# Level products of the gated recurrences as four 64 by 64 tiles

## The chip, the cores and the metric

The kernel runs on one NeuronCore of a Trainium2 chip. The metric is the device time of one execution in microseconds. The core has five engines with in-order instruction queues: TensorE (PE; its weight loads are shown apart as PEld), VectorE (DVE), ScalarE (ACT), GpSimd (POOL) and SyncE (SP), which issues most of the DMAs.

## What is computed

One layer of a decoder trunk over 2048 tokens of width 1024, in f32: a token mixer (three groups of heads in parallel), then a gated MLP with a short convolution, each between an adaLN-conditioned RMSNorm and a gated residual, and a last RMSNorm. Two of the head groups are gated recurrences, HGRN2 (8 heads, key width 64) and GLA (4 heads, key width 32), with a decay per key channel and token:

```python
def step(s, inp):                       # one chunk of tokens
    qn, kn, vn, gn = inp                # gn: log of the decay
    cum = jnp.cumsum(gn, axis=2)
    rel = jnp.where(causal, cum[:, :, :, None, :] - cum[:, :, None, :, :], -jnp.inf)
    attn = jnp.einsum('bhid,bhjd,bhijd->bhij', qn, kn, jnp.exp(rel))
    o = jnp.einsum('bhij,bhje->bhie', attn, vn) + jnp.einsum('bhid,bhde->bhie', qn * jnp.exp(cum), s)
    last = cum[:, :, -1:, :]
    s_new = jnp.exp(last[:, :, 0, :])[..., None] * s + jnp.einsum('bhjd,bhje->bhde', kn * jnp.exp(last - cum), vn)
    return s_new, o
```

The third group, retention (4 heads, key width 64), has a fixed decay per head.

## The kernel before

Tokens are worked in four blocks of 512 (`TB`), each as four chunks of 128 (`NCH`). Projections, the output projection and the MLP are products in three passes over a high and a low part of each operand (`split3`, lines 256 to 258); they make up most of TensorE's queue. The mixer's recurrences are woven into that queue by hand. A `Clock` counts the microseconds of TensorE work that the program has emitted so far (`adv`), and a recurrence is a generator that yields how many microseconds of other work should come before its next step. `clock.chain` runs such generators one after another. Within one engine the order is the order of emission, except that `tc.high_priority(offset=n)` moves instructions ahead by n places in the count of instructions.

`gated` is the generator for one unit: two HGRN2 heads (`unit_h`, 4 units a block, 16 in all) or the four GLA heads (`unit_g`, 1 a block, 4 in all; two "subs" of two heads that share keys and decays). Channels lie on the 128 partitions, 64 for each of two heads, tokens along the free axis. The decayed scores inside a chunk are built by levels. First, pairs of neighbouring tokens (`near`, `dots`). Then for each span s = 2, 4, 8, 16, 32, 64 (`LEVELS`) the scores of the tokens in the second half of each block of 2s against the keys of its first half: a product, a masked copy of it into the score tile `at` (line 679 on VectorE for s up to 16, line 676 on ScalarE above), and a multiplication of the queries (line 668) and the keys (line 670) by the decay of the span. The queries and keys thus change between levels, and the next level's product waits for both.

A level's product (line 660) is one f32 matmul for each chunk: 128 keys as weights, all 128 channels contracted, and as moving operand the queries of half the tokens for both heads side by side, 128 columns. To keep the heads apart the query tile `qbd` has double width and block-diagonal content: `[P, 2, TB]`, where GpSimd clears the half that belongs to the other head (`new_qbd`, lines 532 and 534). For GLA the rows outside the sub's heads are cleared too. After the last level ScalarE copies the second head's rows into the first half (line 691), so that `q[:, 0, :]` holds both heads for the product with the state (line 592).

Scores go to PSUM banks of the tag `lev`, of which there are two. An HGRN2 level writes one bank, a GLA level two, one for each sub. The retention units (`retention`) use the same tag, with one bank for each head, and products over 64 partitions (line 899). They also take their query tile from the tag `qbd`. `kT`, `u` and the outputs use the tag `late`, projections the tag `acc`.

Of the kernel before, what the change touches and what calls it, by code (L numbers as in the profile page):

```python
# [10 lines left out]
F32 = mybir.dt.float32  # L11
# [4 lines left out]
ALU = mybir.AluOpType  # L16
PSUM = bass.MemoryType.PSUM

P = 128
# [3 lines left out]
TB = 512  # L23
NB = SEQ // TB
NCH = TB // P
# [18 lines left out]
M_AT = {2: M_2, 4: M_4, 8: M_8, 16: M_16}  # L44
# [8 lines left out]
M512, M256, MF = 0.227, 0.12, 0.224  # L53
# [5 lines left out]
class Clock:  # L59
# [15 lines left out]
    def adv(self, us):  # L75
        self.t += us
        while self.due and self.due[0][0] <= self.t:
            self._next()
# [26 lines left out]
def trunk(ctx, tc, xT, vecs, cvec, cst, rope, msk, wada, win, walow, wgla, wout, wup, wdown, out):  # L105
# [14 lines left out]
    adv = clock.adv  # L120
# [4 lines left out]
    def lev_ps(name):  # L125
        return pp.tile([P, 512], F32, tag="lev", name=name, bufs=2)
# [133 lines left out]
    h = [None] * KD  # L260
# [264 lines left out]
                low(t[:], k)  # L525


    def new_qbd(name, rows):

        q = p1.tile([P, 2, TB], F32, tag="qbd", name="qb" + name, bufs=3)  # L530
        for hh in range(2):
            G.memset(q[64 * hh:64 * hh + 64, 1 - hh, :], 0.0)
            if rows[hh][1] - rows[hh][0] < 64:
                G.memset(q[64 * hh:64 * hh + 64, hh, :], 0.0)
        return q

    states = [p1.tile([P, NS, P], F32, tag=f"S{i}", name=f"S{i}") for i in range(7)]
    for st in states:
# [88 lines left out]
    def gated(name, b, ui, pos, kq, decay, subs, xy):  # L627

        Sst = states[ui]
        tree, cur = decay  # L630
        two = len(subs) > 1
        nh = 2 * len(subs)
        dots = pu.tile([P, NCH * nh, 2], F32, tag="dots", name="dot" + name, bufs=3)
        pss = [lev_ps(f"dt{name}_{t}") for t in range(2)]
        for ps, x in zip(pss, xy):
            for c in range(NCH):
                T.transpose(ps[:, c * P:(c + 1) * P], x[:, c * P:(c + 1) * P], ident)
        attns = []
        with tc.high_priority(offset=CHAIN):
            for t, ps in enumerate(pss):  # L640
                V.tensor_reduce(dots[:, :, t], ps[:].rearrange("p (a d) -> p a d", a=NCH * nh),  # L641
                                axis=mybir.AxisListType.X, op=ALU.add)
            for i, _ in enumerate(subs):
                at = pa.tile([P, 8 * P], F32, tag="a4k", name=f"at{name}_{i}")
                d8 = dots[:].rearrange("p (a i) t -> p a i t", i=len(subs))[:, :, i, :]
                mk = m_all[:, M_PAIR:M_PAIR + P].bitcast(F32).rearrange("p (n t) -> p n t", t=2)
                V.tensor_tensor(at[:].rearrange("p (a n t) -> p a n t", a=8, t=2),
                                d8.unsqueeze(2).to_broadcast([P, 8, 64, 2]),
                                mk.unsqueeze(1).to_broadcast([P, 8, 64, 2]), op=ALU.mult)
                attns.append(at)  # L650
        adv(4 * MF)
        yield PAIR_GAP
        for li, s in enumerate(LEVELS):
            nb = 64 // s
            pss = []
            for q, rows, v, sg in subs:
                ps = lev_ps(f"lv{name}_{s}")
                for c in range(NCH):
                    rhs = q[:, :, c * P:(c + 1) * P].rearrange("p h (n t s) -> p h n t s", t=2, s=s)[:, :, :, 1, :]
                    T.matmul(ps[:, c * P:(c + 1) * P].rearrange("p (h n s) -> p h n s", h=2, s=s),  # L660
                             kq[:, c * P:(c + 1) * P], rhs, start=True, stop=True)
                pss.append(ps)
            with tc.high_priority(offset=CHAIN):
                ev = tree[li]
                nn = TB // (2 * s)
                for q, rows, v, sg in subs:
                    qv = q[:].rearrange("p h (n t s) -> p h n t s", t=2, s=s)[:, :, :, 1, :]
                    V.tensor_tensor(qv, qv, ev[:, :, 0:1].unsqueeze(1).to_broadcast([P, 2, nn, s]), op=ALU.mult)
                kv = kq[:].rearrange("p (n t s) -> p n t s", t=2, s=s)[:, :, 0, :]
                V.tensor_tensor(kv, kv, ev[:, :, 1:2].to_broadcast([P, nn, s]), op=ALU.mult)  # L670
                for ps, at in zip(pss, attns):
                    dst = at[:].rearrange("p (a n t s) -> p a n t s", a=8, t=2, s=s)[:, :, :, 1, :]
                    src = ps[:].rearrange("p (a n s) -> p a n s", a=8, s=s)
                    if s >= 32:
                        for j0 in range(0, P, 2 * s):
                            S.copy(dst[j0:j0 + s, :, j0 // (2 * s), :], src[j0:j0 + s, :, j0 // (2 * s), :])
                    else:
                        mk = m_all[:, M_AT[s]:M_AT[s] + nb].unsqueeze(2).to_broadcast([P, nb, s])
                        V.copy_predicated(dst, mk.unsqueeze(1).to_broadcast([P, 8, nb, s]), src)
            adv(4 * len(subs) * MF)  # L680
            yield LEVEL_GAP[two]
        ps = late_ps("kT" + name)
        nk = NCH if b < NB - 1 else NCH - 1
        for c in range(nk):
            T.transpose(ps[:, c * P:(c + 1) * P], kq[:, c * P:(c + 1) * P], ident)
        kT = pu.tile([P, NCH, P], F32, tag="kT", name="kT" + name, bufs=1)
        with tc.high_priority(offset=CHAIN):
            S.copy(kT[:, 0:nk, :].rearrange("p c n -> p (c n)"), ps[:, 0:nk * P])
            for q, rows, v, sg in subs:
                r0, r1 = rows[1]  # L690
                S.copy(q[r0:r1, 0, :], q[r0:r1, 1, :])
        adv(4 * MF)
        yield 2.8 if two else 1.8
        while name not in tokens:
            yield 1.0
        for q, rows, v, sg in subs:
            ps = late_ps("u" + name)
            for c in range(nk):
                T.matmul(ps[:, c * P:(c + 1) * P], kT[:, c, :], v[:, c, :], start=True, stop=True)
            with tc.high_priority(offset=CHAIN):  # L700
                for c in range(nk):
                    for hh, (r0, r1) in enumerate(rows):
                        es = slice(64 * hh, 64 * hh + 64)
                        dst = Sst[r0:r1, (b * NCH + c + 1) % NS, es]
                        u = ps[r0:r1, c * P + hh * 64:c * P + hh * 64 + 64]
                        if b == 0 and c == 0:
                            V.tensor_copy(dst, u)
                        else:
                            V.scalar_tensor_tensor(dst, Sst[r0:r1, (b * NCH + c) % NS, es], cur[r0:r1, c:c + 1], u,
                                                   op0=ALU.mult, op1=ALU.add)  # L710
        adv(4 * len(subs) * MF)
        yield 4.0 if two else 2.2
        os = []
        for i, ((q, rows, v, sg), at) in enumerate(zip(subs, attns)):
            if i:
                yield 2.2
            o = pu.tile([P, NCH, P], F32, tag="o", name=f"o{name}_{i}")
            ps = attn_out(f"{name}_{i}", b, at, v, q[:, 0, :], Sst)
            adv(12 * MF)
            with tc.high_priority(offset=CHAIN):  # L720
                S.copy(o[:].rearrange("p c e -> p (c e)"), ps[:])
                post(o, sg, f"{name}_{i}")
            os.append(o)
        yield None
        for i, o in enumerate(os):
            yield 3.0 if i else POST_GAP
            transposed(b, pos + i, o, f"{name}_{i}")
            adv(4 * MF)
# [4 lines left out]
    def unit_h(b, u, pos, between=None):  # L733
# [14 lines left out]
            V.tensor_tensor(sq[:], ps[:], sq[:], op=ALU.mult)  # L748
        xy = near(sq, kq, f, nm)
        rows = [(0, 64), (64, 128)]  # L750
        q = new_qbd(nm, rows)
        for hh, (r0, r1) in enumerate(rows):
            V.tensor_tensor(q[r0:r1, hh, :], sq[r0:r1, :], f[r0:r1, :], op=ALU.mult)
        decay = decays(f, e)
        subs = [(q, rows, *tok_tiles(nm))]
        clock.chain(gated(nm, b, u, pos, kq, decay, subs, xy), {(0, 0): 9.0, (1, 0): 20.0}.get((b, u), 6.0))
# [25 lines left out]
    def unit_g(b, pos):  # L782
# [30 lines left out]
        subs = []  # L813
        for i in range(2):
            rows = [(32 * i, 32 * i + 32), (64 + 32 * i, 96 + 32 * i)]
            q = new_qbd(f"{nm}_{i}", rows)
            for hh, (r0, r1) in enumerate(rows):
                V.tensor_tensor(q[r0:r1, hh, :], qs[r0:r1, :], f[r0:r1, :], op=ALU.mult)
            subs.append((q, rows, *tok_tiles(f"{nm}_{i}")))
        clock.chain(gated(nm, b, 4, pos, kq, decay, subs, xy), 14.0)  # L820
        pss = tf512(f"vg{nm}", 18)
# [6 lines left out]
    def unit_r(b, r, pos):  # L828
# [4 lines left out]
        cos, sin = (rots[b][:, :, i, :] for i in range(2))  # L833
        kk = pu.tile([P, NCH, P], F32, tag="e", name="kk" + nm)
        kc = pu.tile([P, TB], F32, tag="k", name="kc" + nm, bufs=3)
        q = p1.tile([P, 2, TB], F32, tag="qbd", name="qb" + nm, bufs=3)[:, 0, :]
        vsg = tok_tiles(nm)
        pss = tf512("qkvg" + nm, 22 + 4 * r)
        a, bb = ([tmp(f"{n}{i}{nm}") for i in range(2)] for n in ("ra", "rb"))
# [21 lines left out]
    def retention(nm, b, r, pos, a, kk, kc, q, vsg):  # L861
# [8 lines left out]
        qn = pu.tile([P, TB], F32, tag="f", name="qn" + nm, bufs=3)  # L870
        with tc.high_priority(offset=CHAIN):
            S.copy(kc[:], kps[:])
            S.copy(q, qps[:])
            S.activation(qn[:], qps[:], AF.Copy, scale=gc)
        ps = late_ps("u" + nm)
        nk = NCH if b < NB - 1 else NCH - 1
# [789 lines left out]
```

## Time and profile before

| | |
|---|---|
| time before | 2501.42 us, median of 3 runs (2498.31 to 2505.31) |
| the profiled execution | 2501.14 us, span 2499.4 us |
| granted TensorE clock, mean | 0.996 |
| PE busy | 2439.9 us, 98% of the span, 12237 matmul records |
| DVE, ACT, POOL busy | 1884.6, 1200.6, 142.8 us |
| DMA | 525.10 MB, mean 210 GB/s |
| level products on PE (line 660) | 768 records in HGRN2 units, 384 in GLA units |
| masked copies on DVE (line 679) | 64 in HGRN2 units, 32 in GLA units |

The profile is of one execution; times in it are microseconds from the start of the span unless marked ns. L660 is line 660 of the kernel. A row of a group gives line, engine, operation, output and inputs by name, the shape, the count, then busy time and mean length of one, and the idle time of the engine before them with what ended it. A row of the timeline gives start, length, engine, line and operation; `128*128` is the rows and columns of the array that a product uses. Rows of one line give the lengths in ns as least/median/most. Matmuls are pipelined, so that their lengths overlap; how far apart they start is the better measure.

### The profile page before, as it was taken

Reading aid. Unit: us, or ns where it says so; the run is one execution under the profiler, and the core shown is the slowest. Engines: PE = TensorE matmul, PEld = TensorE weight load, DVE = VectorE, ACT = ScalarE, POOL = GpSimd, SP = SyncE. Lnnn points to the kernel's source line nnn. Section 1 sums busy time; section 2 is a strip of 40 time slices with the busy share of each in tenths; the row PEclk is TensorE's granted clock in tenths of the full one; section 3 lists DMA queues with packets and bytes.
Section 4 is the critical chain, followed back from the end, with each engine's and each line's share of the span. In section 5 each row is a group of like instructions: output and inputs, shape, how many; then the busy total and the mean of one; then the engine's idle time right before and its main releaser. Section 6 shows DMA issues by size and latency. Waiting matters only on the chain.

```text
span 2499.4 us, 34934 instructions
## 1 busy us (share of the span) xinstructions
PE 2439.9 (98%) x12237; PEld 2049.9 (82%) x12237; DVE 1884.6 (75%) x3335; ACT 1200.6 (48%) x2034; POOL 142.8 (6%) x262
## 2 busy tenths in 40 slices
PE   5999999999999999999999999999999999999998
PEld 4888788888888888888788888888878888888887
DVE  7987787867588685867787877777787777777666
ACT  4444435535454444434655454555445454555453
POOL 1000000000000000000100000000011110110000
PEclk9999999999999999999999999999999999999999
DMA  8843559864689647985654444487665444447663
GB/s 309 308 160 135 171 181 331 312 208 167 222 301 317 210 160 257 313 309 173 223 190 163 137 163 156 154 289 243 212 214 184 148 152 144 148 136 269 207 193 133
DMA packets 232496, 525.10 MB, mean 210 GB/s; under 512 B 24928, under 2 KB 28032, under 8 KB 232320
## 3 DMA queue, kind: packets, MB, share of 16 engines
q1 hardware_dynamic: 229120, 512.38, 61.0%
q0 software_dynamic: 3200, 10.49, 1.2%
q8 instruction: 96, 1.57, 0.3%
q14 instruction: 80, 0.66, 0.1%
HBM read 397.46 MB, written 125.30 MB: 209 GB/s over the span
## 4 chain that ended last, share of the span: by engine, by line
PE 46%; DMA 2%; DVE 2%; issue 1%; ACT 1%; POOL 0%; DVEq 0%; POOLq 0%; SPq 0%; ACTq 0%
PE X L256 6%; PE X L258 6%; PE X L257 6%; PE Z L258 3%; PE Z L257 3%; PE Z L256 3%; PE dX L256 3%; PE dX L258 3%; PE dX L257 3%; PE dY L257 2%; PE dY L256 2%; PE dY L258 2%; PE Y L258 1%; PE Y L257 1%; PE Y L256 1%
## 5 line engine op out<-in xcount | busy, mean ns | idle before, releaser
L256 PE MATMUL X<-B,A 128*128 128x512 f32 x572 | 223.8, 391 | 4.5 <-ACT u L1357 2.8
L257 PE MATMUL X<-B,A 128*128 128x512 f32 x572 | 223.0, 390 | 0.0
L258 PE MATMUL X<-B,A 128*128 128x512 f32 x572 | 222.9, 390 | 0.0
L1061 DVE TENSOR_TENSOR dA<-rd,dA 128x512 fp32r<-128x512 f32 x154 | 105.8, 688 | 89.8 <-ACT dA L1060 89.5
L1060 ACT CAST dA<-rd 128x512 fp32r<-128x512 f32 x154 | 95.5, 620 | 138.6 <-PE dY L258 47.1
L1061 DVE TENSOR_TENSOR A<-s,A 128x512 fp32r<-128x512 f32 x176 | 120.7, 686 | 49.0 <-ACT A L1060 46.0
L256 PE MATMUL dX<-dB,dA 128*128 128x512 f32 x352 | 137.0, 389 | 0.7 <-DVE uv L1313 0.7
L1060 ACT CAST A<-s 128x512 fp32r<-128x512 f32 x176 | 108.6, 618 | 59.1 <-PE Z L258 45.1
L257 PE MATMUL dX<-dB,dA 128*128 128x512 f32 x352 | 136.9, 389 | 0.0
L258 PE MATMUL dX<-dB,dA 128*128 128x512 f32 x352 | 136.9, 389 | 0.0
L256 PEld LDWEIGHTS X<-B,A 128*128 128x128 f32 x572 | 107.6, 188 | 28.4 <-ACT u L1357 3.2
L258 PEld LDWEIGHTS X<-B,A 128*128 128x128 f32 x572 | 107.6, 188 | 22.4
L257 PEld LDWEIGHTS X<-B,A 128*128 128x128 f32 x572 | 107.7, 188 | 22.3
L256 PE MATMUL Z<-B,A 128*128 128x512 f32 x308 | 119.8, 389 | 0.0
L257 PE MATMUL Z<-B,A 128*128 128x512 f32 x308 | 119.8, 389 | 0.0
L258 PE MATMUL Z<-B,A 128*128 128x512 f32 x308 | 119.8, 389 | 0.0
L1061 DVE TENSOR_TENSOR dB<-rb,dB 128x512 fp32r<-128x512 f32 x154 | 104.9, 685 | 9.1 <-ACT dB L1060 9.0
L660 PEld LDWEIGHTS lvh<-qbh,kh 128*128 128x128 f32 x768 | 99.7, 190 | 13.4 <-issue 5.6
L1060 ACT CAST A<-r 128x512 fp32r<-128x512 f32 x130 | 81.1, 624 | 61.4 <-PE Z L258 59.2
L256 PE MATMUL psqkvgr<-hqkvgr,ha 128*128 128x512 f32 x256 | 106.1, 414 | 0.0
L660 PE MATMUL lvh<-qbh,kh 128*128 128x128 f32 x768 | 102.1, 275 | 3.1 <-DVE doth L641 1.3
L1060 ACT CAST dB<-rb 128x512 fp32r<-128x512 f32 x154 | 94.7, 617 | 17.4 <-DMA rb<-gs 15.2
(473 smaller groups left out, 6884.6 us busy)
## 6 DMA issues: line engine op xcount, KB each, us to landing
gs<-yv SPq DMA_DIRECT2D x154, 256.0 KB, 2.5
rb<-gs SPq DMA_DIRECT2D x154, 256.0 KB, 4.0
r<-wup SPq DMA_DIRECT2D x140, 256.0 KB, 3.2
s<-sumsu SPq DMA_DIRECT2D x136, 256.0 KB, 2.9
wada<-wada SPq DMA_DIRECT2D x48, 512.0 KB, 6.5
rd<-sumsd SPq DMA_DIRECT2D x88, 256.0 KB, 3.8
rd<-wdown SPq DMA_DIRECT2D x66, 256.0 KB, 3.7
x<-xT SPq DMA_DIRECT2D x64, 256.0 KB, 5.7
```

Source lines behind the costliest of these rows:

```text
L256: T.matmul(ps, lhs[0], rhs[0], start=first, stop=False, skip_group_check=more)
L257: T.matmul(ps, lhs[0], rhs[1], start=False, stop=False, skip_group_check=more)
L258: T.matmul(ps, lhs[1], rhs[0], start=False, stop=last, skip_group_check=more)
L660: T.matmul(ps[:, c * P:(c + 1) * P].rearrange("p (h n s) -> p h n s", h=2, s=s), kq[:, c * P:(c + 1) * P], rhs, start=True, stop=True)
L1060: S.copy(hi, src)
L1061: V.tensor_tensor(lo, src, hi, op=ALU.subtract)
```

## The change

The query tile gets single width, `[P, TB]`, with both heads' channels on their own partitions and nothing to clear for HGRN2; for GLA the rows of the other sub's heads are cleared. A level's product becomes, for each chunk, four matmuls on quarters of the array: 64 channels (one head) by 64 keys, with 64 moving columns. At span 64 only the first 64 keys are multiplied. Each head's scores lie in a bank of its own, so an HGRN2 level takes both `lev` banks; in GLA the two subs share each bank, 256 columns each. The multiplication of the queries by the decay covers half as many columns. A score copy is made for each head, so twice as many of half the width. The copy at line 691 goes away. The query tag has four buffers where there were three of twice the size, and the clock is advanced by 3 or 5 times `MF` (0.224) for a level instead of 4 or 8.

```diff
-    def new_qbd(name, rows):
-
-        q = p1.tile([P, 2, TB], F32, tag="qbd", name="qb" + name, bufs=3)
-        for hh in range(2):
-            G.memset(q[64 * hh:64 * hh + 64, 1 - hh, :], 0.0)
-            if rows[hh][1] - rows[hh][0] < 64:
-                G.memset(q[64 * hh:64 * hh + 64, hh, :], 0.0)
-        return q
+    def new_q(name):
+        return p1.tile([P, TB], F32, tag="q", name="q" + name, bufs=4)
...
         for li, s in enumerate(LEVELS):
             nb = 64 // s
-            pss = []
-            for q, rows, v, sg in subs:
-                ps = lev_ps(f"lv{name}_{s}")
+            pss = [lev_ps(f"lv{name}_{s}_{hh}") for hh in range(2)]
+            for i, (q, rows, v, sg) in enumerate(subs):
                 for c in range(NCH):
-                    rhs = q[:, :, c * P:(c + 1) * P].rearrange("p h (n t s) -> p h n t s", t=2, s=s)[:, :, :, 1, :]
-                    T.matmul(ps[:, c * P:(c + 1) * P].rearrange("p (h n s) -> p h n s", h=2, s=s),
-                             kq[:, c * P:(c + 1) * P], rhs, start=True, stop=True)
-                pss.append(ps)
+                    for hh, ps in enumerate(pss):
+                        hs = slice(64 * hh, 64 * hh + 64)
+                        rhs = q[hs, c * P:(c + 1) * P].rearrange("p (n t s) -> p n t s", t=2, s=s)[:, :, 1, :]
+                        for k0 in range(0, P if s < 64 else 64, 64):
+                            n0 = 256 * i + 64 * c
+                            T.matmul(ps[k0:k0 + 64, n0:n0 + 64].rearrange("p (n s) -> p n s", s=s),
+                                     kq[hs, c * P + k0:c * P + k0 + 64], rhs, start=True, stop=True)
             with tc.high_priority(offset=CHAIN):
...
                 for q, rows, v, sg in subs:
-                    qv = q[:].rearrange("p h (n t s) -> p h n t s", t=2, s=s)[:, :, :, 1, :]
-                    V.tensor_tensor(qv, qv, ev[:, :, 0:1].unsqueeze(1).to_broadcast([P, 2, nn, s]), op=ALU.mult)
+                    qv = q[:].rearrange("p (n t s) -> p n t s", t=2, s=s)[:, :, 1, :]
+                    V.tensor_tensor(qv, qv, ev[:, :, 0:1].to_broadcast([P, nn, s]), op=ALU.mult)
...
-                for ps, at in zip(pss, attns):
-                    dst = at[:].rearrange("p (a n t s) -> p a n t s", a=8, t=2, s=s)[:, :, :, 1, :]
-                    src = ps[:].rearrange("p (a n s) -> p a n s", a=8, s=s)
-                    if s >= 32:
-                        for j0 in range(0, P, 2 * s):
-                            S.copy(dst[j0:j0 + s, :, j0 // (2 * s), :], src[j0:j0 + s, :, j0 // (2 * s), :])
-                    else:
-                        mk = m_all[:, M_AT[s]:M_AT[s] + nb].unsqueeze(2).to_broadcast([P, nb, s])
-                        V.copy_predicated(dst, mk.unsqueeze(1).to_broadcast([P, 8, nb, s]), src)
-            adv(4 * len(subs) * MF)
+                for i, at in enumerate(attns):
+                    for hh, ps in enumerate(pss):
+                        dst = at[:].rearrange("p (c h n t s) -> p c h n t s", c=NCH, h=2, t=2, s=s)[:, :, hh, :, 1, :]
+                        src = ps[:, 256 * i:256 * i + 256].rearrange("p (c n s) -> p c n s", c=NCH, s=s)
+                        if s >= 32:
+                            for j0 in range(0, P, 2 * s):
+                                S.copy(dst[j0:j0 + s, :, j0 // (2 * s), :], src[j0:j0 + s, :, j0 // (2 * s), :])
+                        else:
+                            mk = m_all[:, M_AT[s]:M_AT[s] + nb].unsqueeze(2).to_broadcast([P, nb, s])
+                            V.copy_predicated(dst, mk.unsqueeze(1).to_broadcast([P, NCH, nb, s]), src)
+            adv((2 * len(subs) + 1) * MF)
...
-            for q, rows, v, sg in subs:
-                r0, r1 = rows[1]
-                S.copy(q[r0:r1, 0, :], q[r0:r1, 1, :])
...
-        q = new_qbd(nm, rows)
-        for hh, (r0, r1) in enumerate(rows):
-            V.tensor_tensor(q[r0:r1, hh, :], sq[r0:r1, :], f[r0:r1, :], op=ALU.mult)
+        q = new_q(nm)
+        V.tensor_tensor(q[:], sq[:], f[:], op=ALU.mult)
...
-            q = new_qbd(f"{nm}_{i}", rows)
-            for hh, (r0, r1) in enumerate(rows):
-                V.tensor_tensor(q[r0:r1, hh, :], qs[r0:r1, :], f[r0:r1, :], op=ALU.mult)
+            q = new_q(f"{nm}_{i}")
+            for r0, r1 in rows:
+                n0 = r0 + 32 - 64 * i
+                G.memset(q[n0:n0 + 32, :], 0.0)
+                V.tensor_tensor(q[r0:r1, :], qs[r0:r1, :], f[r0:r1, :], op=ALU.mult)
...
-        q = p1.tile([P, 2, TB], F32, tag="qbd", name="qb" + nm, bufs=3)[:, 0, :]
+        q = new_q(nm)
```

More of the change, by code (lines that the diff above doesn't have):

```diff
@@ L717, in gated @@
             o = pu.tile([P, NCH, P], F32, tag="o", name=f"o{name}_{i}")
-            ps = attn_out(f"{name}_{i}", b, at, v, q[:, 0, :], Sst)
+            ps = attn_out(f"{name}_{i}", b, at, v, q, Sst)
             adv(12 * MF)
@@ L872, in retention @@
             S.copy(kc[:], kps[:])
-            S.copy(q, qps[:])
+            S.copy(q[:], qps[:])
             S.activation(qn[:], qps[:], AF.Copy, scale=gc)
```

## The prediction

> **What bounds the kernel now.** I read the page from the top: busy shares, the slices, the chain that ended last; then the stretch in which the changed lines run.
>
> ```profile
> span 2499.4 us, 34934 instructions
> PE 2439.9 (98%) x12237; PEld 2049.9 (82%) x12237; DVE 1884.6 (75%) x3335; ACT 1200.6 (48%) x2034; POOL 142.8 (6%) x262
> PEclk9999999999999999999999999999999999999999
> PE 46%; DMA 2%; DVE 2%; issue 1%; ACT 1%; POOL 0%; DVEq 0%; POOLq 0%; SPq 0%; ACTq 0%
> ```
> TensorE is busy 98% of the span at full clock, and the chain names it far ahead of any other engine. The level products (line 660) run between 70 and 1160 us, the token mixer. That window alone:
> ```profile
> 70.00:1160.00 1090.00, 1080.41 (x6079) 923.54 (x6078) 832.41 (x1810) 490.34 (x925) 32.73 (x64) 1.00 0.69 236
> ```
> Columns after the length: PE, PEld, DVE, ACT, POOL busy. PE is idle 9.6 us of 1090, so there a microsecond taken from PE's queue is a microsecond of span, and VectorE's 832 us matter only where PE waits for them. Each f32 product is two records (a weight load and a matmul, twice).
> ```profile
> L660 PE MATMUL lvh<-qbh,kh 128*128 128x128 f32 x768 | 102.1, 275 | 3.1 <-DVE doth L641 1.3 <-DVE kh L670 1.1 <-DVE nw L159 0.3
> L660 PE MATMUL lvg<-qbg,kg 128*128 128x128 f32 x384 | 46.8, 274 | 0.0
> ```
> 768 records are 16 units of the HGRN2 group (h) x 6 levels x 8; 384 are 4 units of the GLA group (g) x 6 x 16. The 275 ns are a pipelined latency; what a group costs is read from the timeline, by how far it pushes its neighbours apart.
> ```profile
> 424.30 0.39 PE L258 MATMUL psvgg<-hvgg,ha 128*128 128x512 f32 x1
> 424.53 1.05 PE L660 MATMUL lvh<-qbh,kh 128*128 128x128 f32 x8
> 425.34 0.48 PE L256 MATMUL psvgg<-hvgg,ha 128*128 128x512 f32 x1
> 425.65 0.40 PE L257 MATMUL psvgg<-lvgg,ha 128*128 128x512 f32 x1
> 425.88 0.39 PE L258 MATMUL psvgg<-hvgg,ha 128*128 128x512 f32 x1
> ```
> ```profile
> 449.66 0.39 PE L258 MATMUL pshfh<-ha,lhfh 128*128 128x512 f32 x1
> 449.88 1.95 PE L660 MATMUL lvg<-qbg,kg 128*128 128x128 f32 x16
> 451.90 0.40 PE L257 MATMUL pshfh<-ha,hhfh 128*128 128x512 f32 x1
> ```
> Projection products start 0.23 us apart (425.65 to 425.88). From 424.30 to 425.65 are 1.35 us, two products explain 0.46, so an h level costs 0.89 us, 0.111 a record. A g level costs 2.24 - 0.46 = 1.78. In all 96 x 0.89 + 24 x 1.78 = 128 us of PE.
>
> **The change part by part. PE products.** An h level becomes 16 products of 64 rows, 64 weight columns and 64 moving columns (32 records), at span 64 only 8 (16 records); g has twice that. The trace has no product on a quarter of the array. The nearest is the retention score, two row halves (64*128), each head in its own bank:
> ```profile
> 322.00 0.39 PE L258 MATMUL pshfh<-ha,lhfh 128*128 128x512 f32 x1
> 322.31 1.16 PE L899 MATMUL scr<-qbr,kcr 64*128 64x128 f32 x16
> 323.41 0.50 PE L256 MATMUL pshfh<-ha,hhfh 128*128 128x512 f32 x1
> 323.74 0.39 PE L257 MATMUL pshfh<-ha,hhfh 128*128 128x512 f32 x1
> ```
> ```profile
> 323.40 0.19 PEld L256 LDWEIGHTS pshfh<-ha,hhfh 128*128 128x128 f32 x1
> 323.51 0.19 PEld L257 LDWEIGHTS pshfh<-ha,hhfh 128*128 128x128 f32 x1
> ```
> The stage costs 1.74 - 0.46 = 1.28 us for 16 records. One after another at 0.111 they would take 1.78, and the last would start 1.67 after the first; the row covers 1.16 and a matmul lasts 0.27, so it starts 0.89 after. Two tiles do run at a time: 8 steps x 0.111 = 0.89. The other 0.39 us is the way into and out of the divided array: no load under the last product before, none under the last score, two bare 128-column loads (0.11 each, 323.40 to 323.51).
>
> How a record shrinks with its width:
> ```profile
> 412.49 1.02 PE L802 MATMUL zg<-alg,gup 128*128 128x512 f32 x2
> ```
> ```profile
> L802 PE MATMUL zg<-alg,gup x8: 592/592/595, 106.1 to 994.6; 128*128 128x512 f32 x8
> ```
> ```profile
> 86.68 0.19 PEld L258 LDWEIGHTS psvgh<-hvgh,ha 128*128 128x128 f32 x1
> 86.80 0.11 PEld L789 LDWEIGHTS alg<-ha,alow 128*32 128x32 f32 x1
> ```
> Two f32 records of 512 columns start 0.43 apart (1.02 less one record's 0.59 us), four times 0.107; 96 weight columns less save 0.08 us, 0.053 for 64. So load and matmul of 64 columns each take half, 0.056 a step, and the bare load on the way in is 0.055 instead of 0.11: the way in and out is 0.34.
>
> The open quantity is how many of the four tiles run together. Bounds from rows: four (every tile a stream, as the two were), 14 ns a record; two, 28 ns; no overlap, 56 ns, the score's mean distance between starts. I take four: row halves, whose records also stand in the queue half after half, showed complete overlap, and nothing in those rows limits two streams. Then:
> - h level: 0.34 + 8 x 0.056 = 0.79, saves 0.10; span 64: 0.34 + 4 x 0.056 = 0.56, saves 0.33. A unit saves 5 x 0.10 + 0.33 = 0.83; 16 units 13.3 us.
> - g level: 0.34 + 16 x 0.056 = 1.24, saves 0.54; span 64: 0.79, saves 0.99. A unit saves 3.7; 4 units 14.8 us.
> Together -28 us.
>
> **VectorE, ScalarE, GpSimd.**
> ```profile
> L668 DVE TENSOR_TENSOR qbh<-qbh,eh x80: 672/685/695, 83.4 to 1151.7; 128x512 f32<-128x512 f32 x80
> ```
> ```profile
> L670 DVE TENSOR_TENSOR kh<-kh,eh x80: 405/418/421, 84.0 to 1152.9; 128x256 f32<-128x256 f32 x80
> ```
> ```profile
> L679 DVE COPY_PREDICATED ath<-m_all,lvh x64: 695/710/1324, 79.4 to 1143.7; 128x512 f32<-128x512 uint32 x64
> ```
> ```profile
> L691 ACT COPY qbh<-qbh x16: 616/617/619, 102.3 to 1152.6; 64x512 f32<-64x512 f32 x16
> ```
> The query product halves, 685 to 418 ns, in 144 calls: -38 us of DVE. Slope 1.04 ns a column leaves 0.15 us fixed, so a masked copy split in two costs about +0.15, x96: +14. The h query start is one 128-row product instead of two of 64 rows (16 x 0.69: -11). DVE -35 us. ScalarE loses 24 copies of 0.617 (-15 us) and has its score copies split; GpSimd zeroes less. All this lies under PE, whose idle time in the window bounds any gain at 9.6 us; I count 0. If that cover went, it would not cost but give. The shorter clock advances and the larger count of instructions reorder the queues (a priority offset counts instructions); I see no sign to give it: 0, with the same 9.6 us as its gain and 3.7 us as its loss, one more stall like the largest of this stretch, at a block's start:
> ```profile
> L257 PE MATMUL pshfh<-ha,hhfh 128*128 128x512 f32 x112 | 44.5, 398 | 3.7 <-DVE ha L373 3.7
> ```
>
> **The added wait.** An h level used one of the two score banks, so level n+1 wrote while n was being copied. Now each level takes both, and its first products wait for n's masked copies; behind them stands the whole in-order PE queue. The copies usually end before, but not where VectorE is behind:
> ```profile
> 79.45 1.30 DVE L679 COPY_PREDICATED ath<-m_all,lvh 128x512 f32<-128x512 uint32 x1
> ...
> 79.67 1.13 PE L660 MATMUL lvh<-qbh,kh 128*128 128x128 f32 x8 [0.38 <-DVE kh L670]
> ```
> ```profile
> 1097.99 0.70 DVE L679 COPY_PREDICATED ath<-m_all,lvh 128x512 f32<-128x512 uint32 x1
> 1098.22 0.46 PE L660 MATMUL lvh<-qbh,kh 128*128 128x128 f32 x2
> ```
> ```profile
> 338.11 1.15 PE L660 MATMUL lvh<-qbh,kh 128*128 128x128 f32 x8 [1.06 <-DVE doth L641]
> 339.61 0.68 DVE L641 TENSOR_REDUCE doth<-dth 128x8 f32<-128x512 f32 x1
> ```
> These are the first and last of 13 such transitions among 80 (1.08 and 0.47 us over), 9.4 us in all, and one of two units whose second pair sum still holds the other bank (2.2, and 1.1 at 74.57). The copies end about 0.12 earlier than before (0.27 won, 0.15 lost): 8 + 3 = 11 us at most. A wait lets VectorE catch up, so neighbours do not all pay; 0 is the other end, and I take 7. In g both banks were always taken.
>
> **Sum.** -28 + 7 = -21 on the profiled execution's 2501.1 us (span 2499.4 plus 1.7), which lies at the median of the runs, 2501.4: 2480.
>
> **The rivals.** *Two at a time* (slower). Column halves of the array share their rows' stream, so only row halves overlap and a start comes every 28 ns. For it: the trace shows two streams, never four. Against: nothing held them back. An h level is 0.34 + 0.90 = 1.24 (+0.35), span 64 0.79 (-0.10), a unit +1.6, 16 units +26; g +0.35 and -0.54, 4 units +5; with the waits +38: 2539. The point of decision is 0.89: an h level breaks even at 17 ns a record. The Trainium skill, page "TensorE: Matmul & The Clock Gate", section "Wait — 56ns, not 53.3ns?", says that matmuls never start closer than about 25 ns however narrow. By it an h level's 32 records take 0.80 us and the sum would be an estimated 2526; the score's starts, 56 ns apart on average, do not test it.
>
> *No overlap*: 56 ns a record gives h 2.13 (+1.24), a unit +6.6, 16 units +105; g 4 x 11.1 = +44; with the waits 2657. Only two streams' overlap speaks against it.
>
> *Eaten by the banks* (no change). If a half-width masked copy costs as much as a whole one (0.70, and 1.30 at span 2), 29 transitions overshoot, 27 us, with the pair sums 30: -28 + 30, 2503. Against: at full width the copy's 0.70 is the product's 0.685, which does shrink.
>
> **How the numbers follow.** Four tiles 0.57, its own range 2467 to 2490: waits 0 to 11, and 0.05 us either way on 120 ways in and out, 6 us. Fewer, up to two at a time 0.26; no overlap 0.05; eaten 0.12. The range to 2542 (two at a time, waits of 11) leaves out no overlap and the edges, about 1 in 10. Faster by over 0.3% (7.5 us, about what runs of this kernel tell from no change) 0.59: four tiles and a little of the second; same 0.13; slower 0.28.
>
> **What would show it.** On the timeline an h level of spans 2 to 32 should push its neighbours apart by 0.8 us, at span 64 by 0.56, g by 1.24; 1.24 for h says two at a time, over 2 none. Query products at 0.42, masked copies at 0.43 twice. Waits of the level products on the masked copy's tile should sum to 3 to 11 us; PE idle in the mixer above 40 us would mean that the banks decide. The forecast is wrong if the column halves do not overlap, or the way in and out costs well over 0.34.

## The result, and the profile after

The changed kernel takes 2523.91 us (median of 6 runs, 2519.55 to 2532.83) against 2500.59 for the kernel before: 1.0095 times as long, 95% interval 1.0082 to 1.0108, or 23.8 us slower by that ratio, where 2480 was forecast. The profiled execution is the longest of the six, 2532.83 us; what is read from its trace belongs to the 31.7 us by which it is longer than the profiled execution before, not to the 23.8.

The page of the changed kernel: span, busy times and instruction counts, and the chain that ended last, by engine.

```profile
span 2530.7 us, 41217 instructions
PE 2442.9 (97%) x15309; PEld 2009.1 (79%) x15309; DVE 1844.3 (73%) x3415; ACT 1191.3 (47%) x2082; POOL 119.4 (5%) x214
PE 45%; DMA 2%; DVE 2%; issue 1%; ACT 0%; SPq 0%; POOL 0%; DVEq 0%; POOLq 0%; ACTq 0%
```

VectorE lost 40 us, ScalarE 9, GpSimd 23: VectorE's part is near the 35 of the forecast. The operations shrank as forecast: at the median a query product takes 0.42 us, and a masked copy 0.43, twice. TensorE's busy time did not fall, though the products got cheaper, and the span grew. The window of the mixer, 70 to 1160 us, in the same columns as before:

```profile
70.00:1160.00 1090.00, 1056.38 (x8983) 861.21 (x8982) 779.98 (x1860) 470.56 (x942) 10.96 (x21) 0.99 0.69 233
```

TensorE is now idle 33.6 us of 1090 where it was 9.6, and its mean clock is no longer 1.00. The level products themselves, on the timeline (start, length):

```profile
421.97 0.39 PE L258 MATMUL psvgg<-hvgg,ha 128*128 128x512 f32 x1
422.29 0.69 PE L657 MATMUL lvh<-qh,kh 64*64 64x64 f32 x32
422.92 0.50 PE L256 MATMUL psvgg<-hvgg,ha 128*128 128x512 f32 x1
423.26 0.39 PE L257 MATMUL psvgg<-lvgg,ha 128*128 128x512 f32 x1
...
426.23 0.39 PE L258 MATMUL psvgg<-hvgg,ha 128*128 128x512 f32 x1
426.55 0.68 PE L657 MATMUL lvh<-qh,kh 64*64 64x64 f32 x16
427.16 0.50 PE L256 MATMUL psvgg<-hvgg,ha 128*128 128x512 f32 x1
427.50 0.39 PE L257 MATMUL psvgg<-lvgg,ha 128*128 128x512 f32 x1
...
444.23 0.39 PE L258 MATMUL psvgg<-hvgg,ha 128*128 128x512 f32 x1
444.55 1.17 PE L657 MATMUL lvg<-qg,kg 64*64 64x64 f32 x64
445.66 0.50 PE L256 MATMUL psvgg<-hvgg,ha 128*128 128x512 f32 x1
445.99 0.40 PE L257 MATMUL psvgg<-lvgg,ha 128*128 128x512 f32 x1
```

Read as before, less 0.46 for two projection products: an h level pushes its neighbours 0.83 us apart, an h level of span 64 takes 0.81, a g level 1.30. Now the waits of TensorE: who waited, for whom, then the total in us, how often, and the longest.

```profile
PE lvg L657 <- DVE atg L676: 7.0, 9, 1.8
...
PE psvgh L256 <- DVE sqh L742: 5.4, 3, 3.9
PE or L588 <- DVE atr L898: 4.3, 6, 1.4
...
PE lvh L657 <- DVE doth L635: 3.4, 1, 3.4
...
PE lvh L657 <- DVE ath L676: 2.5, 5, 0.8
```

In the kernel before, these places read as follows; level products waited for no masked copy there.

```profile
PE lvh L660 <- DVE doth L641: 1.3, 2, 1.1
PE or L594 <- DVE atr L903: 1.2, 2, 0.8
...
PE psvgh L256 <- DVE sqh L748: 0.2, 1, 0.2
```

Two kinds of waits have come: level products behind the masked copies (7.0 us in g, 2.5 in h), which are the banks; and waits in places that the change does not touch in the code, the projections' `psvgh` behind the queries' gate `sqh` (0.2 to 5.4) and the retention outputs behind their masked scores `atr` (1.2 to 4.3). At the medians read from all 120 level groups, the products cost 109 us where they cost 128; with the waits among them they push their neighbours apart by 136.0 us in all, against 135.0 before. So the whole gain of the products is given back inside the level groups, and the rest is lost beside them.

What a wait costs is more than its length. Windows around the longest of the `sqh` waits (columns as above, the granted clock third from the end), then the products in them:

```profile
480.50:483.93 3.43, 1.39 (x19) 0.85 (x15) 0.68 (x1) 2.55 (x6) 0.00 (x0) 1.00 1.04 391
483.93:490.76 6.83, 5.02 (x12) 3.97 (x13) 6.37 (x13) 1.67 (x2) 0.00 (x0) 0.50 0.84 324
490.76:494.17 3.41, 3.41 (x19) 2.79 (x18) 0.81 (x2) 0.25 (x1) 0.00 (x0) 1.00 0.57 134
```

```profile
481.50 0.39 PE L258 MATMUL psvgh<-hvgh,ha 128*128 128x512 f32 x1
485.74 0.80 PE L256 MATMUL psvgh<-hvgh,ha 128*128 128x512 f32 x1 [3.85 <-DVE sqh L742]
486.34 0.63 PE L257 MATMUL psvgh<-lvgh,ha 128*128 128x512 f32 x1
486.76 0.63 PE L258 MATMUL psvgh<-hvgh,ha 128*128 128x512 f32 x1
...
490.91 0.40 PE L256 MATMUL psvgh<-hvgh,ha 128*128 128x512 f32 x1
```

After 3.85 us of idle time the products start 0.42 apart instead of 0.23, until 490.76. Between 60 us and 30 us before the end the trace before has 10.2 us at half clock, that of the changed kernel 44.4, which costs up to (44.4 - 10.2) / 2 = 17 us.

### The profile page after: what moved, and what is told of

It is laid out like the page before. It is cut to its first block, busy times and chain, and to the rows that moved or that the text cites. A ratio compares the mean times of both kernels' runs of the same rounds, so it can differ in the third digit from the quotient of the medians.

```text
span 2530.7 us, 41217 instructions
## 1 busy us (share of the span) xinstructions
PE 2442.9 (97%) x15309; PEld 2009.1 (79%) x15309; DVE 1844.3 (73%) x3415; ACT 1191.3 (47%) x2082; POOL 119.4 (5%) x214
## 4 chain that ended last, share of the span: by engine, by line
PE 45%; DMA 2%; DVE 2%; issue 1%; ACT 0%; SPq 0%; POOL 0%; DVEq 0%; POOLq 0%; ACTq 0%
PE X L256 6%; PE X L257 6%; PE X L258 6%; PE Z L257 3%; PE Z L258 3%; PE Z L256 3%; PE dX L256 3%; PE dX L258 3%; PE dX L257 3%; PE dY L256 2%; PE dY L258 2%; PE dY L257 2%; PE Y L257 1%; PE Y L258 1%; PE Y L256 1%
## 5 line engine op out<-in xcount | busy, mean ns | idle before, releaser
L256 PE MATMUL psvgh<-hvgh,ha 128*128 128x512 f32 (+1 forms) x256 | 100.8, 394 | 5.4 <-DVE sqh L742 5.4
L1056 DVE TENSOR_TENSOR A<-r,A 128x512 fp32r<-128x512 f32 x130 | 89.3, 687 | 21.1 <-ACT A L1055 20.6
```

The costliest lines, as they stand in the source:

```text
L256: T.matmul(ps, lhs[0], rhs[0], start=first, stop=False, skip_group_check=more)
L1056: V.tensor_tensor(lo, src, hi, op=ALU.subtract)
```

## The experiments

The ratios are to the kernel before on the same chip, run beside each set; its median was 2499.83 to 2502.75 us there. "Idle" is TensorE's idle time between 70 and 1160 us in the profiled execution.

| run | median us | ratio to before (95%) | idle us |
|---|---|---|---|
| before | 2500.59 | 1 | 9.6 |
| changed kernel | 2523.91 | 1.0095 (1.0082 to 1.0108) | 33.6 |
| before_split_copies | 2505.48 | 1.0015 (1.0006 to 1.0025) | 14.5 |
| before_two_banks | 2512.14 | 1.0036 (1.0025 to 1.0047) | 17.0 |
| before_new_advance | 2513.21 | 1.0036 (1.0019 to 1.0054) | 16.4 |
| before_longer_advance | 2509.80 | 1.0038 (1.0024 to 1.0052) | 17.0 |
| after_old_advance | 2511.31 | 1.0043 (1.0023 to 1.0064) | 26.0 |
| after_measured_advance | 2511.52 | 1.0038 (1.0020 to 1.0056) | 29.5 |
| after_other_banks | 2537.16 | 1.0135 (1.0120 to 1.0150) | 49.0 |
| tiles_in_g_only | 2508.25 | 1.0033 (1.0019 to 1.0047) | 23.5 |
| tiles_in_h_only | 2519.04 | 1.0068 (1.0053 to 1.0083) | 23.8 |
| tiles_wide_queries | 2535.07 | 1.0133 (1.0112 to 1.0153) | 38.8 |
| after_key_on_gpsimd | 2517.47 | 1.0060 (1.0041 to 1.0079) | 28.3 |
| after_old_advance_first | 2514.69 | 1.0059 (1.0043 to 1.0076) | 24.4 |
| g_only_first | 2509.13 | 1.0029 (1.0016 to 1.0042) | 22.8 |
| after_longer_gaps | 2524.59 | 1.0097 (1.0080 to 1.0114) | 32.7 |
| after_longer_g_gap | 2524.59 | 1.0101 (1.0080 to 1.0122) | 30.3 |
| g_only_longer_gap | 2514.35 | 1.0055 (1.0040 to 1.0070) | 24.6 |

Theories at the start: the banks (a level waits for the copies of the one before), the weave (the shorter clock advance put other work in a worse order), and the order of the other queues.

**The clock advance, in both kernels.** In the changed kernel it is put back, in the kernel before it is shortened; each alone.

```diff
-            adv((2 * len(subs) + 1) * MF)
+            adv(4 * len(subs) * MF)
```

> The changed kernel with the planner's clock advance of a level as it was before (4 MF a sub-unit instead of 2 a sub-unit and 1). TensorE's order is then entry for entry that of the kernel before. Weave theory: the loss goes and the products' gain shows, 2480 to 2500. Bank theory: the waits stay, at most 5 us away from the changed kernel, 2519 to 2529.

> The kernel before with the planner's clock advance of a level as the change has it, and nothing else; TensorE's order is then that of the changed kernel. Weave theory: 15 to 25 us slower than before, 2516 to 2526. Bank theory: within 5 us of before, 2496 to 2506.

Both results lie between the ranges of the two theories. The old advance gives back 1.0095 - 1.0043 = 13 us of the changed kernel's loss, the new one costs the kernel before 9. So about half of the loss is no matter of products, banks or queries, but of two numbers in the planner's clock. The new waits in the kernel before lie in three or four places:

```profile
PE lvh L660 <- DVE doth L641: 4.1, 1, 4.1
...
PE og L592 <- DVE S L709: 3.0, 1, 3.0
...
PE psvgh L256 <- ACT hvgh L307: 2.5, 1, 2.5
...
PE oh L592 <- DVE S L707: 2.1, 1, 2.1
```

A level product, two outputs behind the state, a projection behind its weights: single stalls of 2 to 4 us, not one mechanism repeated. Both forms of the weave theory were tried next.

**Is it that the advance is too short?** First the changed kernel, then the kernel before:

```diff
-            adv((2 * len(subs) + 1) * MF)
+            adv(1.30 if two else 0.82)
...
-            adv(4 * len(subs) * MF)
+            adv(5 * len(subs) * MF)
```

> The changed kernel with the clock advance of a level set to what its products were measured to push their neighbours (0.82 us for h, 1.30 for g, against 0.67 and 1.12 in the changed kernel). TensorE's order is within a few entries that of before. Weave theory, in the form that an advance below the true cost makes the order worse: as the changed kernel with the old advance, 2505 to 2516. In the form that any new order costs about the same by chance: anywhere from 2505 to 2530.

> The kernel before with a clock advance of 5 MF a sub-unit instead of 4, an error of the other sign than in the run with the change's advance. If only a too short advance costs: 2497 to 2507. If any departure from the order that stood costs (the order was fitted to these durations): 2508 to 2525, with new single stalls of 2 us and more, each followed by a half-clock stretch.

With the products' true cost as advance the changed kernel stands where it stands with the old one, and TensorE's order is all but that of before. A longer advance costs the kernel before as much (9.5 us) as the shorter (9.0). So "too short" falls: of the three orders tried the one that stood was the best, and one departure to each side cost the same.

The run with the measured advance also shows what the half clock costs. Its idle time in the mixer is close to that of the changed kernel (29.5 against 33.6 us), but it has 13.7 us at half clock against 44.4, and its profiled execution is 21 us shorter (2511.52 against 2532.83); (44.4 - 13.7) / 2 = 15 of these are the half clock.

**The second bank, and its control.** In the kernel before an h level's products go to two banks, and the copies are split with them (in h `nb2` is 2, in g 1); the control has the same copies, but `[lev_ps(f"lv{name}_{s}")] * nb2`, one bank under both names.

```diff
-                ps = lev_ps(f"lv{name}_{s}")
+                nb2 = 1 if two else 2
+                ps = [lev_ps(f"lv{name}_{s}_{j}") for j in range(nb2)]
...
-                    T.matmul(ps[:, c * P:(c + 1) * P].rearrange("p (h n s) -> p h n s", h=2, s=s),
+                    T.matmul(ps[c * nb2 // NCH][:, c * P:(c + 1) * P].rearrange("p (h n s) -> p h n s", h=2, s=s),
```

> The kernel before, with one edit: an h level's whole-width products go to two level banks (chunks 0 and 1, chunks 2 and 3) and each score copy is split in two; products, query width and TensorE's order stay. Bank theory: each h level now waits for the copies of the level before, 13 of 80 transitions overshot by 9.4 us and the copies end 0.15 us later, so 10 to 25 us slower than before, 2510 to 2525, with waits of the level products on the masked copies' tile of 5 us or more. Other theories: at most 4 us slower (the added VectorE time lies under TensorE), 2497 to 2505.

> The control for the two-bank run: the kernel before with each h score copy split in two as there, but with the products in one bank a level as before. TensorE's order is that of before; VectorE gets 64 short copies more (0.15 us each, 10 us of its 1885). Bank theory: the 9.4 us of the two-bank run came from the second bank, so this one stands within 4 us of before, 2498 to 2505. Order theory (any edit that re-sorts VectorE's queue costs some 8 to 10 us): 2508 to 2514.

2512 us lies inside the range of the bank theory, but the control shows that not all of it is the bank. Two banks cost 9 us and the split copies alone 4, so the second bank costs about 5, with intervals that just touch (1.0025). The waits in the run with two banks:

```profile
PE lvh L661 <- DVE doth L641: 3.2, 4, 1.5
...
PE lvh L661 <- DVE ath L683: 1.8, 3, 1.0
```

1.8 us on masked copies and, against before, 1.9 more on the pair sums: the bank theory names the right place and half the size, and its 5 us of waits on the copies did not come.

**Other banks for every second level**, in the changed kernel:

```diff
-            pss = [lev_ps(f"lv{name}_{s}_{hh}") for hh in range(2)]
+            pss = [(lev_ps if li % 2 else late_ps)(f"lv{name}_{s}_{hh}") for hh in range(2)]
```

> The changed kernel, with one edit: levels of spans 2, 8 and 32 take the two score banks of the retention and state products instead of the level banks, so that consecutive levels never share a bank. The order of TensorE's queue is the same as in the changed kernel. Bank theory (each level waits for the copies of the level before, and the g levels too): the waits of level products on masked copies (7.0 us in g, 2.5 in h) and on the pair sums (3.4) go, and with them part of the half-clock stretches: 13 to 25 us faster than the changed kernel, 2499 to 2511. Weave theory (the shorter clock advance put the work in a worse order): nothing changes, 2519 to 2529. Order theory (VectorE's and the DMA queue's orders moved): nothing systematic, within 10 us of 2524.

All three theories missed: it is slower by another 1.0135 - 1.0095 = 10 us. The tag `late` that the levels borrow is not that of the retention scores, as the expectation has it, but that of `kT`, `u` and the outputs.

```profile
PE lvg L657 <- DVE oTh L576: 16.6, 4, 5.3
...
PE lvh L657 <- DVE oTg L576: 6.3, 4, 2.4
PE oTr L571 <- DVE ath L676: 5.8, 1, 5.8
...
PE lvh L657 <- DVE oTh L576: 3.1, 1, 3.1
```

The level products' waits on masked copies and on the pair sums are gone, as the bank theory had it, but the banks taken instead are those of the output transposes, which ScalarE and then VectorE empty late (lines 574 and 576): 26.0 us of waits for 12.9 removed. An output transpose (`oTr`) now waits for a level's copies in its turn. So this run moves the shared banks to another place; levels that share no bank with anything were not run.

**One kind of unit at a time**, in the kernel before with its advance, so that TensorE's order is that of before. `tiles` chooses between the old and the new lines of a level; in g alone it is `two`, in h alone `not two`.

```diff
+        tiles = two
...
+            if tiles:
+                pss = [lev_ps(f"lv{name}_{s}_{hh}") for hh in range(2)]
...
+            else:
                 pss = []
```

> The kernel before with the four tiles and single-width queries in the GLA units only; the HGRN2 units keep their whole-width products in one bank each; the clock advance is that of before, so TensorE's order is that of before. Products at the durations seen in the changed kernel: 20 levels x 0.49 + 4 x 0.57 = 12 us less of TensorE. Bank theory: the g levels' waits on masked copies (6.4 us with the old advance) take about half of that, 2493 to 2501. If GLA carries the loss (waits followed by half-clock stretches): 2502 or more. If no wait mattered: 2488 to 2491.

> The kernel before with the four tiles and single-width queries in the HGRN2 units only; the GLA units keep their products; old clock advance, TensorE's order of before. Products: 80 x 0.075 + 16 x 0.085 = 7 us less of TensorE. Bank theory: the two-bank hold costs h what it cost with whole-width products, 9 us, so 2500 to 2508. If h's waits are not the loss: 2494 to 2498. The two one-sided kernels together should explain the 9 us that the changed kernel with the old advance lies above before.

In g alone the 12 us of cheaper products end in 8 us of loss, as was expected if the waits of g carry a loss; in h alone 7 us end in 17, outside both ranges. The level products' own waits explain part of either; g alone, then h alone:

```profile
PE lvg L668 <- DVE atg L687: 5.2, 7, 1.5
```

```profile
PE ssn L339 <- DVE S L744: 4.7, 1, 4.7
...
PE or L597 <- DVE atr L937: 3.9, 7, 0.8
...
PE lvh L668 <- DVE doth L645: 2.4, 2, 2.0
...
PE lvh L668 <- DVE ath L687: 2.0, 4, 0.8
```

In g the copies hold up 5.2 us. In h they hold up 2.0, and the state (`S`), the retention's masked scores (`atr`) and the pair sums (`doth`) 11.0: VectorE comes late to work outside the levels. The two losses do not add up (8 + 17 against 11 with both): these stalls do not come by the piece. One difference was not parted: both one-sided kernels keep three query buffers, where the changed kernel has four.

**Tiles without the single-width queries.** The kernel before with the changed kernel's products (from `q[hs, hh, ...]` of the block-diagonal tile) and its split copies:

```diff
-                    rhs = q[:, :, c * P:(c + 1) * P].rearrange("p h (n t s) -> p h n t s", t=2, s=s)[:, :, :, 1, :]
+                        rhs = q[hs, hh, c * P:(c + 1) * P].rearrange("p (n t s) -> p n t s", t=2, s=s)[:, :, 1, :]
```

> The kernel before with only the products changed: four 64 by 64 tiles, each head's scores in a bank of its own, score copies split with them; the queries stay block-diagonal and their products double width, the advance as before. It parts the tiles from the single-width queries, whose VectorE saving (38 us) re-sorted VectorE's queue the most. Order theory (the shorter query products re-sort the queue and so cost): the tiles alone give 2500 (before) - 19 (products) + 5 to 9 (second bank and split copies) and some waits of g = 2490 to 2500. Cover theory (VectorE's load sets how long a level's copies hold the banks, so wide queries make it worse): slower than the changed kernel with the old advance, 2514 to 2530.

The order theory falls. The cover theory has the direction; at 2535 us the run lies 5 us above even its range. It is 1.0133 against 1.0043 with single-width queries, 22 us for 36 us more of VectorE in the mixer window (822.59 against 786.66 busy).

```profile
PE lvh L663 <- DVE ath L682: 5.7, 7, 2.1
PE or L594 <- DVE atr L906: 5.0, 5, 2.2
PE kTh L688 <- DVE kh L672: 4.6, 4, 2.1
```

With single-width queries and the same advance the h waits on masked copies were 1.2 us, those of the retention outputs 3.7, those of the key transposes 2.3. With both banks held and shorter products to hide under, VectorE's work in a level is on the path. Two things were not parted from this. The wide tile keeps three buffers, the narrow one has four; VectorE's waits for a free query tile, 0.5 us in all as in the kernel before, do not show that this matters. And ScalarE keeps its 24 copies of the queries (line 691 before), 15 us of its time.

**VectorE's order and VectorE's load.** The chain's priority reach doubled, in the changed kernel with the old advance and in g alone; then, in the former, the key product on GpSimd:

```diff
-CHAIN = 400
+CHAIN = 800
...
-                V.tensor_tensor(kv, kv, ev[:, :, 1:2].to_broadcast([P, nn, s]), op=ALU.mult)
+                G.tensor_tensor(kv, kv, ev[:, :, 1:2].to_broadcast([P, nn, s]), op=ALU.mult)
```

> The changed kernel with the old advance, and the priority reach of the recurrence's chain doubled (400 to 800 instructions), so that VectorE takes the chain's products and copies ahead of other work; TensorE's order stays that of before. If the waits are VectorE taking the level's copies and the retention's masks late: they halve and the products' 19 us begin to show, 2492 to 2504. If what moves forward only makes other stalls: 2507 to 2520.

> The tiles in the GLA units only, with the same doubled reach. As above: if VectorE's order was what ate the products' 12 us, 2490 to 2498; if it makes other stalls, 2502 to 2515.

> The changed kernel with the old advance, and the key product of every level (0.42 us on VectorE) moved to GpSimd, which is 5% busy, so that a level's queries and copies on VectorE end about 0.4 us earlier. If what is left of the loss is VectorE taking a level's work too late: 2495 to 2506, with shorter waits of the level products on masked copies. If GpSimd takes over 0.9 us for the product, the key becomes the last of a level: 2515 to 2535, with waits on the key's tile by GpSimd.

No priority helps: 1.0059 and 1.0029 against 1.0043 and 1.0033, inside each other's intervals. The key product takes 0.72 us on GpSimd against 0.42 on VectorE:

```profile
L666 POOL TENSOR_TENSOR kh<-kh,eh x80: 615/721/1632, 80.4 to 1165.5; 128x256 f32<-128x256 f32 x80
```

This median is under the 0.9 at which the key was to become the last of a level (35 of all 120 key products took longer than that), and still nothing was won (1.0060; g's wait on copies 8.1 us against 6.4). But VectorE's load hardly fell: its busy time in the mixer window went from 786.66 to 775.60 us, though 120 products of 0.42 us, 50 us, had left it. Its other work got slower; the query products, first with the key product on VectorE, then on GpSimd:

```profile
L664 DVE TENSOR_TENSOR qh<-qh,eh 128x256 f32<-128x256 f32 x80 | 33.5, 419 | 23.4 <-PE lvh L657 23.4
L664 DVE TENSOR_TENSOR qh<-qh,eh 128x256 f32<-128x256 f32 x80 | 39.8, 497 | 25.0 <-PE lvh L657 25.0
```

The mean went from 419 to 497 ns. So the run does not test what a lighter load of VectorE would give.

**More room between levels.** Gaps for h and g; the second run has (3.2, 5.4), and the third, in g alone, (3.2, 5.2).

```diff
-LEVEL_GAP, PAIR_GAP = (3.2, 4.8), 4.0
+LEVEL_GAP, PAIR_GAP = (3.4, 5.2), 4.0
```

> The changed kernel with the old advance and the planner's gap between levels raised from 3.2 to 3.4 us (h) and from 4.8 to 5.2 (g), so that other products lie longer between a level and the one that needs its banks. If VectorE's lateness against a fixed gap is the rest of the loss: the g levels' waits on masked copies fall from 6.4 us to under 4 and the time to 2495 to 2506. If the order that stood is what counts and every shift makes stalls elsewhere: 2508 to 2522.

> As the run above, with the gap raised for the GLA units only, from 4.8 to 5.4 us. Lateness: the g waits (6.4 us) fall below 3, 2500 to 2506. Order: 2508 to 2522.

> The tiles in the GLA units only, with their gap raised from 4.8 to 5.2 us. The products save 12 us and the waits on copies were 6 us: 2494 to 2500 if the gap removes them, 2504 to 2512 if they come back elsewhere.

All three are slower than with the old gaps, by 6 to 15 us, and 2 to 3 us beyond even the range of the second theory. g's waits on copies stayed at 6.1 and 6.4 us; in g alone they fell from 5.2 to 3.9, and an h level met 4.1 us on the pair sums instead. No version with the tiles was faster than the kernel before.

## Why the prediction was wrong

**Product term, -28 us: the mechanism right, the size off.** All four tiles run together: h 0.83 against the forecast 0.79, g 1.30 against 1.24, far from the 1.24 and over 2 that the first two rivals gave for h. What failed first is the step "span 64: 0.34 + 4 x 0.056". There only the first 64 keys are multiplied, so two of the four tiles have work, and 16 records in two tiles take 8 steps like 32 in four: 0.81 instead of 0.56, in g 1.22 to 1.28 where nothing stood in the way, instead of 0.79. With the measured costs the term is 80 x 0.07 + 16 x 0.085 + 20 x 0.49 + 4 x 0.5 = 19 us. So 9 us of the forecast were never there: some 6 of them at span 64, the rest in the way in and out, which costs a few hundredths of a microsecond a level more than the 0.34.

**Wait term, +7 us: too small, and one step false.** "In g both banks were always taken" is true and says nothing. Before, a g bank held one sub and came free with one copy; now it holds one head of both subs, and the first bank waits for three of the four copies. g's waits on masked copies, forecast at none, are 7.0 us; those of h, where the 7 was expected, 2.5. The 3.4 on the pair sums, a single wait at 335 us, cannot be put down to the banks: with the shorter advance alone, the kernel before has 4.1 us there, at 337 us. The sum on masked copies, 9.5, lies inside the 3 to 11 that was to be seen by luck, since most of it is in g.

**"All this lies under PE": false.** As the runs have it, VectorE's work was covered by the alternation of banks and by the length of the products, and the change takes the first and shortens the second. The queries' saving, counted at 0, is worth 22 us once the tiles stand: without it, and with the old advance, the tiles made the kernel 33 us slower.

**Reorder at 0, "no sign to give it": the largest miss of a single term.** The advance alone is 13 us in the changed kernel, 9 in the kernel before, more than the 3.7 that was the bound of its loss. The sign could have been given: a hand-fitted order with 9.6 us of idle time in 1090 has little left to gain from a shift and any stall to lose.

**A price that was not in the sum.** Each wait was counted at its length. The half-clock stretches behind them add up to 17 us in the profiled execution.

Together for that execution: TensorE's idle time over the whole span rose by 28 us (59.5 to 87.8) and its busy time by 3 (2439.9 to 2442.9). In the busy time the products' -19 and up to 17 of half clock meet, which would give -2. So some 5 us of busy time are not placed; waits shorter than the 0.27 us that a matmul's length covers would lie there, for they do not show as idle time, but this was not followed up.

**The rivals.** "Two at a time" and "no overlap" are refuted by the 0.83. That 2524 lies below the 2542 to which the range reached is luck: the range reached there for two tiles at a time, which did not happen. The Trainium skill, page "TensorE: Matmul & The Clock Gate", section "Wait — 56ns, not 53.3ns?", has starts never closer than about 25 ns; the trace disagrees for records on different tiles, since 32 more records make a g level 1.30 - 0.83 = 0.47 us longer than an h level, 15 ns each. "Eaten by the banks" is the nearest in mechanism, but at 2503 it had neither the advance nor the price of a stall, and idle time in the mixer stayed at 33.6 us, under the 40 that were to show that the banks decide.

**What stays open.** With the old advance, the changed kernel's 11 us of loss stand against 19 of gain, so 30 us of new cost; the second bank and the split copies in h account for 9 of it, if they cost with tiles what they cost in the kernel before. What the traces show of the rest is mostly VectorE coming late: in the changed kernel VectorE ended 21 stalls of TensorE of over 0.5 us between 60 and 1200 us, and through 20 of them it worked without a pause of more than 0.15 us. The wide queries show that more load makes this worse; how much of it is load and how much the order of VectorE's queue is not shown, since each edit moves both. The one exception is the longest of them, the 3.85 us behind `sqh`. There VectorE stood still itself:

```profile
481.42 0.60 ACT L740 ACTIVATE sqh<-pshqh 128x512 f32<-128x512 f32 x1
```

```profile
480.49 0.69 DVE L360 TENSOR_TENSOR san<-san,sqn 128x512 f32<-128x512 f32 x1 [1.02 <-ACT sqn L359]
484.39 0.69 DVE L941 TENSOR_TENSOR wsd<-wsd 128x512 f32<-128x512 f32 x1 [3.21 <-DMA wsd<-wdown]
485.00 0.68 DVE L742 TENSOR_TENSOR sqh<-pshqh,sqh 128x512 f32<-128x512 f32 x1
```

ScalarE had finished its part of the gate at 482.02. But ahead of the gate's product (line 742) stood, in VectorE's queue, a sum over MLP weights (line 941) that waited 3.21 us for its DMA. So a transfer for a later stage held up a queue that the mixer needed.

## What to carry to other kernels

Where an in-order queue has been fitted by hand to 98% busy, cost an edit by what it does to the fit: the four such edits that were tried in the kernel before cost 4 to 10 us, a longer advance as much as a shorter one. An operation that "lies under" the bound engine does so by a buffer; if the edit also takes the spare buffer, that operation belongs in the sum (here 36 us more of VectorE cost 22). And when tiles of the array are counted on, count for each case how many of them have work.

## What the runs showed of the hardware

The granted clock follows idle time on a fixed grid. In all 18 traces the half-clock stretches start on a raster of 3.413 us and last one, two or three steps of it. Of some 12,570 steps at full clock between 70 us and 30 us before the end, 75 had TensorE idle for over 2.0 us, and all 75 were followed by a step at half clock; with over 1.79 us idle, 83 of 87 were; with under 1.2 us, 3 of some 12,400. So a stall of 2 to 4 us costs itself and up to 1.7 or 3.4 us more, or nothing more where the raster happens to split it: in the kernel before, the stall of 2.79 us that ended at 1226 us had no half-clock step behind it. The Trainium skill, page "TensorE: Matmul & The Clock Gate", section "What's actually happening", gives the raster, free-running, at 3413 ns, which the traces confirm, and has the clock fall after at least one idle window; here a little over half a window was enough.

Four products on quarters of the array that stand one behind the other in the queue do run together: 64 records of 64 columns in 1.30 us, 20 ns each with the way into and out of the divided array.

A product on GpSimd slows the products that VectorE runs beside it. With the key products on GpSimd, the 56 query products of VectorE that had one beside them for at least 30% of their length took 589 ns in the mean, the 88 others 416; with the key products on VectorE they all took 419.
